# Values of four heads as one 512-column group, their gates as the next, with half of the values and results held in DRAM

## The chip, the core and the metric

The kernel runs on one core of a Trainium2 chip, in float32 data (matrix products in the chip's fp32r form, with operands split into a high and a low part). The metric is the device time in microseconds from launch to end. Before the change it is 775.31 us, the median of three runs (775.07 to 775.48).

## The reference

One layer of a mixer. `x` is 512 frames by 2048 channels.

```python
xn = rmsnorm(x, norm_gain)
q, k, v, g_sb, x_lru, g_lru = split(xn @ w_in, 6 parts of 1024 columns)
# 8 heads of 128: QK-norm, stick-breaking attention, strictly causal
w[t, s] = sigmoid(z[t, s]) * prod over s < j < t of (1 - sigmoid(z[t, j]))
y_sb  = (w @ v) * silu(g_sb)
# 8 groups of 128 channels: causal conv of width 4, two gate products, linear recurrence
y_lru = scan(conv(x_lru)) * silu(g_lru)
out = x + concat(y_sb, y_lru) @ w_out
```

## The kernel before, in words

**The loop.** The input projection is done in four rounds, p = 0 to 3, of two heads and two LRU channel groups each (line 528). A round has three groups of matmuls, each made by `in_group` (line 241) into four PSUM banks of the pool `ps_mm`, which has only those four: "qk" (queries and keys of two heads), "xg" (inputs and gates of two LRU groups) and "vg" (values and gates of two heads). A group runs over 8 chunks of the 2048 input channels; a chunk is one weight tile (`load_w`, line 223, two DMAs), split on ScalarE into a high part and on VectorE into a low part (`split_w`), and then three matmuls for each bank and each block of 128 channels: high by high, high by low, low by high.

**The vg group.** For queries, keys and gates the weights are stationary and 512 frames are streamed, so every matmul has 512 columns. Values are wanted with frames on the partitions, so there the frames are stationary and the weights are streamed; of the 512 weight columns of a vg group only 256 are values. So its first two banks are filled by matmuls of 256 columns, two halves to a bank (lines 278 to 289), and the other two banks, the gates, by matmuls of 512 (lines 292 to 294).

**After a vg group.** `finish_vg` (line 509) splits the values straight from PSUM into `vh`, `vl` and `v3` (lines 517 to 520), scales the two gate banks (`evac`, line 351), turns them into silu gates (`silu_gate`: three ScalarE steps, a VectorE step, a ScalarE step and a VectorE step, on one scratch tile `se` that all gates share with those of the LRU groups), makes the product of attention weights and values on TensorE (`attention_values`, lines 443 and 445) and multiplies it by the gate into `y_dram` (`gated`, line 364).

**The end of the loop and the output product.** `finish_vg(3)` and the scan of the last LRU group are put behind the first two weight splits of the output product (line 641). The products of heads 6, 7 and of LRU groups 6, 7 with their gates go straight into the tiles `yl` (line 648). The output product is done in the Strassen manner by seven products, in the order 1, 7, 5, 3, 6, 2, 4, each of 96 matmuls; each wants its weights split (line 619 on ScalarE, 620 on VectorE, 128x1024 at a time). The tiles `yl` go first into the sums for product 5 (lines 744 to 747).

**Order of the work.** Every engine works through its own list in order. The lists are laid out ahead by the framework's planner, which goes by its own estimate of durations and by the order of the program (`schedule_with_timeline_sim=True`); where an instruction waits, everything behind it on that engine waits too. Weight loads and results are issued on the queue of SyncE (SP); DMAs that add weights into DRAM run on the queue of GpSimd.

Of the kernel before, what the change touches and what calls it, by code (L numbers as in the profile page):

```python
# [9 lines left out]
F32 = mybir.dt.float32  # L10
# [12 lines left out]
def hybrid_block_kernel(ctx: ExitStack, tc: tile.TileContext, x, norm_gain, w_in, q_norm_gain,  # L23
# [7 lines left out]
    TT = S // P  # L31
    KC = 2
    WARM = 15
    FILL = 4
# [188 lines left out]
    def load_w(src, name):  # L223
        t = raw_pool.tile([P, KC, 512], F32, tag="raw", name=name)
        for s in range(2):
            last = nc.sync.dma_start(t[:, :, 256 * s:256 * s + 256], src[:, :, s, :])
        return t, last
# [12 lines left out]

    def in_group(a, p, vfirst, name, first=False):
        banks = [ps_mm.tile([P, 512], F32, tag="mm", name=f"{name}b{i}") for i in range(4)]
        NC = KT // KC

        def load(c):
            t, last = load_w(w_in_v[:, KC * c:KC * c + KC, a, :, 256 * p:256 * p + 256], f"{name}r{c}")
            if not first and c % 2 == 1 and sums:
                with tc.issue_after(last.ins):
                    sums.pop(0)()
            return t  # L250
# [8 lines left out]
        for c in range(NC):  # L259
# [13 lines left out]
            for b in range(4):  # L273
                for j in range(KC):
                    kt = KC * c + j
                    st, sp = kt == 0, kt == KT - 1
                    wh, wl = hl[j]
                    if vfirst and b < 2:
                        for u in range(2):
                            tt = 2 * b + u  # L280
                            o = banks[b][:, u * 256:(u + 1) * 256]
                            ts = slice(tt * P, (tt + 1) * P)
                            s0 = st and u == 0
                            nc.tensor.matmul(o, lhsT=xh[kt][:, ts], rhs=wh[:, 0:256], start=s0, stop=False,
                                             skip_group_check=True)
                            nc.tensor.matmul(o, lhsT=xh[kt][:, ts], rhs=wl[:, 0:256], start=False, stop=False,
                                             skip_group_check=True)
                            nc.tensor.matmul(o, lhsT=xl[kt][:, ts], rhs=wh[:, 0:256], start=False, stop=sp,
                                             skip_group_check=True)
                    else:  # L290
                        cs = slice(b * P, (b + 1) * P)
                        nc.tensor.matmul(banks[b], lhsT=wh[:, cs], rhs=xh[kt], start=st, stop=False)  # L292
                        nc.tensor.matmul(banks[b], lhsT=wh[:, cs], rhs=xl[kt], start=False, stop=False)  # L293
                        nc.tensor.matmul(banks[b], lhsT=wl[:, cs], rhs=xh[kt], start=False, stop=sp)  # L294
# [138 lines left out]

    def attention_values(h, wt, v, gate):
        hp = h % 2
# [9 lines left out]
        nc.tensor.matmul(o[:, 384:512], lhsT=v3[:, hs], rhs=w3, start=False, stop=True, skip_group_check=True)  # L445
        gated(h, o, gate)

# [60 lines left out]

    def finish_vg(p, banks, wts):
        vh = v_pool.tile([P, 3, 256], F32R, tag="vh", name=f"vh{p}")  # L510
        vl = v_pool.tile([P, 3, 256], F32R, tag="vl", name=f"vl{p}")
        v3 = v_pool.tile([P, 256], F32, tag="v3", name=f"v3{p}")
        for tt in range(TT):
            src = banks[tt // 2][:, (tt % 2) * 256:(tt % 2) * 256 + 256]
            r = rtok[:, tt:tt + 1]
            if tt == 3:
                nc.scalar.activation(v3, src, AF.Copy, scale=r)
                continue
            nc.scalar.activation(vh[:, tt, :], src, AF.Copy, scale=r)
            nc.vector.scalar_tensor_tensor(out=vl[:, tt, :], in0=src, scalar=r, in1=vh[:, tt, :].bitcast(F32),  # L520
                                           op0=ALU.mult, op1=ALU.subtract)
        v = (vh, vl, v3)
        gs = [evac(banks[2 + i], f"s{2 * p + i}") for i in range(2)]
        gates = [silu_gate(gs[i], f"s{2 * p + i}") for i in range(2)]
        for i in range(2):
            attention_values(2 * p + i, wts[i], v, gates[i])

    for p in range(4):
        banks = in_group(0, p, False, f"qk{p}", p == 0)
        banks = [evac(banks[i], f"qk{p}_{i}") for i in range(4)]  # L530
# [4 lines left out]
        wts = [attention_weights(2 * p + i) for i in range(2)]  # L535
        banks = in_group(2, p, False, f"xg{p}")
        xg = []
# [7 lines left out]
        for i in range(2):  # L545
            scans[i] = lru(2 * p + i, xg[i], xg[2 + i])
            if p < 3 or i == 0:
                scans[i]()
        banks = in_group(1, p, True, f"vg{p}")
        if p < 3:  # L550
            finish_vg(p, banks, wts)

# [88 lines left out]
    with tc.issue_after(last_hi[0].ins), tc.issue_after(last_lo[0].ins):  # L641
        scans[1]()
        finish_vg(3, banks, wts)
    for a in range(2):
        nc.sync.dma_start(yl[a], y_dram_a[1, :, a])
    for k in (14, 6, 15, 7):
        y, gate = late[k]
        nc.vector.tensor_tensor(out=yl[k % 4][:, k // 8], in0=y, in1=gate, op=ALU.mult)

    def product(i, banks, src, w):  # L650
# [171 lines left out]
```

## Time and profile before

| | |
|---|---|
| median of three runs | 775.31 us |
| the profiled execution | 775.84 us, of which the span of the instructions is 774.1 us |
| TensorE busy | 764.6 us |
| VectorE busy | 512.3 us |
| ScalarE busy | 440.5 us |
| DMA | 133.92 MB, mean 173 GB/s |

Times in the rows below count from the first instruction of the span. A duration of a matmul holds its way through the array, and the next one starts before it ends; what a matmul costs in a dense stretch is the distance from its start to the next start.

### The profile page before, as it was taken

The numbers are of one execution on the slowest core, as the hardware profiler recorded it, in microseconds if no ns is written. First come the engines' busy times: TensorE is split into PE (matmuls) and PEld (weight loads), VectorE is DVE, ScalarE is ACT, GpSimd is POOL, SyncE is SP. The second block draws the span as 40 slices with busy tenths as digits, with TensorE's granted clock in tenths as the row PEclk, the third lists the DMA queues.
The fourth block names the chain that finished last, engine by engine and source line by source line (L and its number), as shares of the span: only waits on it lengthen the run. The fifth ranks groups of instructions, "written<-read, shape, count | busy, mean of one in ns | idle before, by whom it ended". The sixth has DMA issues, their size and how long they took to land.

```text
span 774.1 us, 10702 instructions
## 1 busy us (share of the span) xinstructions
PE 764.6 (99%) x3853; PEld 647.5 (84%) x3853; DVE 512.3 (66%) x857; ACT 440.5 (57%) x828; POOL 37.4 (5%) x55
## 2 busy tenths in 40 slices
PE   8999999999999999999999999999999999999997
PEld 6888889988888899888889988888888878788886
DVE  4554587783445797725468976254787889976973
ACT  4934568582245777524469673245786766345541
POOL 0001101010101101001100000000000000000000
PEclk9999999999999999999999999999999999999999
DMA  9677876768987776788787523323145589898811
GB/s 287 208 167 141 198 165 163 172 148 215 185 203 144 197 154 177 148 227 193 164 200 145 149 90 123 108 85 106 55 133 168 151 340 315 227 290 200 262 63 55
DMA packets 92153, 133.92 MB, mean 173 GB/s; under 512 B 6258, under 2 KB 62148, under 8 KB 91844
## 3 DMA queue, kind: packets, MB, share of 16 engines
q1 hardware_dynamic: 83364, 116.45, 48.4%
q0 software_dynamic: 8704, 16.78, 18.1%
q8 instruction: 30, 0.49, 0.3%
q14 instruction: 23, 0.19, 0.1%
q10 hardware_dynamic: 32, 0.01, 0.0%
HBM read 125.87 MB, written 40.89 MB: 215 GB/s over the span
## 4 chain that ended last, share of the span: by engine, by line
PE 93%; DVE 5%; DMA 1%; issue 0%; SPq 0%; ACT 0%; DVEq 0%
PE p L679 5%; PE p L680 5%; PE p L678 5%; PE z L387 4%; PE qk0b L293 2%; PE qk0b L294 2%; PE xg0b L293 2%; PE xg3b L294 2%; PE xg1b L294 2%; PE xg2b L294 2%; PE xg0b L294 2%; PE xg3b L292 2%; PE xg2b L292 2%; PE xg1b L292 2%; PE xg0b L292 2%; PE xg1b L293 2%
## 5 line engine op out<-in xcount | busy, mean ns | idle before, releaser
L679 PE MATMUL p<-wo,os 128*128 128x512 f32 x192 | 74.9, 392 | 0.5 <-DVE wo L620 0.4
L680 PE MATMUL p<-wo,os 128*128 128x512 f32 x192 | 74.5, 390 | 0.0
L678 PE MATMUL p<-wo,os 128*128 128x512 f32 x192 | 69.5, 390 | 0.7 <-ACT wo L619 0.7
L619 ACT CAST wo<-c 128x1024 fp32r<-128x1024 f32 x44 | 46.2, 1051 | 35.6 <-PE p L680 33.9
L620 DVE TENSOR_TENSOR wo<-c,wo 128x1024 fp32r<-128x1024 f32 x44 | 53.4, 1222 | 13.4 <-ACT wo L619 13.4
L309 POOL DMA_DIRECT2D ws<-in_w_out_dram x32 | 33.8, 1055 | 371.4 <-DMA ws<-in_w_out_dram 185.0
L679 PEld LDWEIGHTS p<-wo,os 128*128 128x128 f32 x192 | 36.0, 188 | 9.6 <-DVE wo L620 2.3
L678 PEld LDWEIGHTS p<-wo,os 128*128 128x128 f32 x192 | 36.0, 188 | 8.6 <-ACT wo L619 1.1
L680 PEld LDWEIGHTS p<-wo,os 128*128 128x128 f32 x192 | 36.1, 188 | 7.4
L399 ACT ACTIVATE sp<-z 128x128 f32<-128x128 f32 (+3 forms) x32 | 13.9, 434 | 27.6 <-PE z L387 27.4
L293 PE MATMUL qk0b<-xl,hqk 128*128 128x512 f32 x64 | 26.4, 413 | 0.0
L294 PE MATMUL qk0b<-xh,lqk 128*128 128x512 f32 x64 | 25.2, 394 | 0.0
L293 PE MATMUL xg0b<-xl,hxg 128*128 128x512 f32 x64 | 25.2, 394 | 0.0
L292 PE MATMUL xg1b<-xh,hxg 128*128 128x512 f32 x64 | 25.2, 393 | 0.0
L292 PE MATMUL xg2b<-xh,hxg 128*128 128x512 f32 x64 | 25.2, 393 | 0.0
L292 PE MATMUL xg3b<-xh,hxg 128*128 128x512 f32 x64 | 25.1, 393 | 0.0
L292 PE MATMUL xg0b<-xh,hxg 128*128 128x512 f32 x64 | 25.1, 392 | 0.0
L293 PE MATMUL xg1b<-xl,hxg 128*128 128x512 f32 x64 | 25.1, 392 | 0.0
L293 PE MATMUL xg2b<-xl,hxg 128*128 128x512 f32 x64 | 25.1, 392 | 0.0
L293 PE MATMUL xg3b<-xl,hxg 128*128 128x512 f32 x64 | 25.1, 392 | 0.0
L294 PE MATMUL qk1b<-xh,lqk 128*128 128x512 f32 x64 | 25.0, 391 | 0.0
L292 PE MATMUL qk1b<-xh,hqk 128*128 128x512 f32 x64 | 24.9, 390 | 0.0
(542 smaller groups left out, 2377.4 us busy)
## 6 DMA issues: line engine op xcount, KB each, us to landing
ws<-in_w_out_dram POOLq DMA_DIRECT2D x32, 512.0 KB, 8.4
c<-ws SPq DMA_DIRECT2D x28, 512.0 KB, 5.2
ws<-in_w_out_dram SPq DMA_DIRECT2D x16, 512.0 KB, 6.8
ws<-ws SPq DMA_DIRECT2D x16, 512.0 KB, 6.4
c<-in_w_out_dram SPq DMA_DIRECT2D x16, 512.0 KB, 5.8
qk0r<-in_w_in_dram SPq DMA_DIRECT2D x16, 256.0 KB, 5.1
xg0r<-in_w_in_dram SPq DMA_DIRECT2D x16, 256.0 KB, 4.0
vg0r<-in_w_in_dram SPq DMA_DIRECT2D x16, 256.0 KB, 3.7
```

What stands on the lines that cost most here:

```text
L292: nc.tensor.matmul(banks[b], lhsT=wh[:, cs], rhs=xh[kt], start=st, stop=False)
L293: nc.tensor.matmul(banks[b], lhsT=wh[:, cs], rhs=xl[kt], start=False, stop=False)
L294: nc.tensor.matmul(banks[b], lhsT=wl[:, cs], rhs=xh[kt], start=False, stop=sp)
L309: nc.gpsimd.dma_start(wsum[i, m, a], block(*add, m, a), accum_op=ALU.add)
L387: nc.tensor.matmul(o, lhsT=lhsT, rhs=rhs, start=start, stop=stop, skip_group_check=True)
L399: nc.scalar.activation(e, z, AF.Abs)
L619: last_hi[0] = nc.scalar.copy(h, src)
L620: last_lo[0] = nc.vector.tensor_tensor(out=l, in0=src, in1=h.bitcast(F32), op=ALU.subtract)
L678: nc.tensor.matmul(bank, lhsT=sh[:, j, us], rhs=wh[:, j, :], start=st, stop=False)
L679: nc.tensor.matmul(bank, lhsT=sh[:, j, us], rhs=wl[:, j, :], start=False, stop=False)
L680: nc.tensor.matmul(bank, lhsT=sl[:, j, us], rhs=wh[:, j, :], start=False, stop=sp)
```

## The change

Values and gates of four heads, not two, are now gathered into groups. In round 0 (and 2) the third group is V: 512 columns of values of heads 0 to 3 (4 to 7), frames stationary, all matmuls of 512 columns, one bank to a block of 128 frames. In round 1 (and 3) it is G: the gates of the same four heads. In round 0 the values of heads 2 and 3 are scaled and written to DRAM (`v_dram`), and read back in round 1 before G is computed; the ungated results of heads 0 and 1 are written to DRAM (`o_dram`) and read back in round 1 to be multiplied by their gates. In round 2 the ungated results of heads 4 and 5 go to `y_dram` as they are, and are multiplied by their gates in the tiles `yl` at the end. A V or G weight tile comes by one DMA.

```diff
     def load_w(src, name):
         t = raw_pool.tile([P, KC, 512], F32, tag="raw", name=name)
+        if len(src.shape) == 3:
+            return t, nc.sync.dma_start(t, src)
...
-                    if vfirst and b < 2:
-                        for u in range(2):
-                            tt = 2 * b + u
-                            o = banks[b][:, u * 256:(u + 1) * 256]
-                            ts = slice(tt * P, (tt + 1) * P)
-                            s0 = st and u == 0
-                            nc.tensor.matmul(o, lhsT=xh[kt][:, ts], rhs=wh[:, 0:256], start=s0, stop=False,
-                                             skip_group_check=True)
...
+                    if a == V:
+                        ts = slice(b * P, (b + 1) * P)
+                        nc.tensor.matmul(banks[b], lhsT=xh[kt][:, ts], rhs=wh, start=st, stop=False)
+                        nc.tensor.matmul(banks[b], lhsT=xh[kt][:, ts], rhs=wl, start=False, stop=False)
+                        nc.tensor.matmul(banks[b], lhsT=xl[kt][:, ts], rhs=wh, start=False, stop=sp)
...
+    def finish_v(p, banks, wts):
+        scales = [rtok[:, tt:tt + 1] for tt in range(TT)]
+        v = split_v(p, [b[:, 0:256] for b in banks], scales)
+        for i in range(2):
+            t = wtile(f"vk{p}_{i}")[:, 0:512].rearrange("p (t c) -> p t c", t=2)
+            for u in range(2):
+                nc.scalar.activation(t[:, u, :], banks[2 * i + u][:, 256:512], AF.Copy, scale=scales[2 * i + u])
+            nc.sync.dma_start(v_dram[p // 2, i], t)
+        for i in range(2):
+            h = 2 * p + i
+            o = attention_values(h, wts[i], v)
+            t = y_pool.tile([P, S], F32, tag="y", name=f"o{h}")
+            nc.scalar.copy(t, o)
+            nc.sync.dma_start(o_dram[i] if h < 2 else y_dram[h], t)
+
+    def load_v(p):
+        srcs = []
+        for i in range(2):
+            t = wtile(f"vr{p}_{i}")[:, 0:512].rearrange("p (t c) -> p t c", t=2)
+            nc.sync.dma_start(t, v_dram[p // 2, i])
+            srcs += [t[:, 0, :], t[:, 1, :]]
+        return split_v(p, srcs, [1.0] * TT)
+
+    def finish_g(p, banks, wts, v):
+        gs = [evac(banks[i], f"s{2 * p - 2 + i}") for i in (2, 3, 0, 1)]
+        gates = [silu_gate(g, f"s{p}_{i}") for i, g in enumerate(gs)]
+        for i in range(2):
+            gated(2 * p + i, attention_values(2 * p + i, wts[i], v), gates[i])
+        for i in range(2):
+            h = 2 * p - 2 + i
+            if h > 1:
+                late[h] = gates[2 + i]
+                continue
+            t = y_pool.tile([P, S], F32, tag="y", name=f"or{h}")
+            nc.sync.dma_start(t, o_dram[i])
+            nc.vector.tensor_tensor(out=t, in0=t, in1=gates[2 + i], op=ALU.mult)
+            nc.sync.dma_start(y_dram[h], t)
...
-        banks = in_group(1, p, True, f"vg{p}")
-        if p < 3:
-            finish_vg(p, banks, wts)
+        if p % 2 == 0:
+            finish_v(p, in_group(V, p // 2, f"v{p}"), wts)
+        else:
+            v = load_v(p)
+            banks = in_group(G, p // 2, f"g{p}")
+            if p < 3:
+                finish_g(p, banks, wts, v)
...
         scans[1]()
-        finish_vg(3, banks, wts)
+        finish_g(3, banks, wts, v)
...
+    for k in (4, 5):
+        nc.vector.tensor_tensor(out=yl[k % 4][:, 0], in0=yl[k % 4][:, 0], in1=late[k], op=ALU.mult)
```

`split_v` is the splitting part of `finish_vg`, taken out as a function.

## Rows read from the trace of the kernel before

**Rows 1.** The page: busy time of each engine, and the chain of waits.
```profile
PE 764.6 (99%) x3853; PEld 647.5 (84%) x3853; DVE 512.3 (66%) x857; ACT 440.5 (57%) x828; POOL 37.4 (5%) x55
...
PE 93%; DVE 5%; DMA 1%; issue 0%; SPq 0%; ACT 0%; DVEq 0%
```

**Rows 2.** Waits of PE, whole span: us in total, times, longest us.
```profile
PE qk0b L292 <- DVE hqk L233: 1.8, 1, 1.8
...
PE p L678 <- ACT wo L619: 0.7, 1, 0.7
PE p L679 <- DVE wo L620: 0.4, 1, 0.4
```

**Rows 3.** Instruction groups by form, PE: busy us, mean ns; one value and one gate row.
```profile
L284 PE MATMUL vg0b<-hvg,xh 128*128 128x256 f32 x64 | 18.0, 283 | 0.0
...
L292 PE MATMUL vg0b<-xh,hvg 128*128 128x512 f32 x32 | 12.6, 393 | 0.0
```

**Rows 4.** Timeline of PE in the qk group of round 1: start us, us.
```profile
179.67 0.39 PE L294 MATMUL qk1b<-xh,lqk 128*128 128x512 f32 x1
...
185.79 0.39 PE L294 MATMUL qk1b<-xh,lqk 128*128 128x512 f32 x1
```

**Rows 5.** Timeline of PE, one chunk of the vg group of round 3.
```profile
599.22 0.28 PE L284 MATMUL vg3b<-hvg,xh 128*128 128x256 f32 x1
...
602.10 0.40 PE L292 MATMUL vg3b<-xh,hvg 128*128 128x512 f32 x1
...
604.84 0.28 PE L284 MATMUL vg3b<-hvg,xh 128*128 128x256 f32 x1
```

**Rows 6.** Busy time by stretch: length, PE, PEld, DVE, ACT, POOL, granted clock, DMA share.
```profile
166.00:315.00 149.00, 149.00 (x769) 127.38 (x769) 92.48 (x162) 85.54 (x164) 12.99 (x14) 1.00 0.79 179
...
611.00:637.00 26.00, 25.81 (x119) 21.05 (x117) 23.78 (x35) 17.24 (x27) 0.00 (x0) 1.00 0.93 321
...
637.00:659.00 22.00, 21.69 (x93) 17.42 (x94) 22.00 (x31) 13.91 (x18) 0.00 (x0) 1.00 0.88 299
```

**Rows 7.** Timeline of DVE around the boundary from round 1 to round 2.
```profile
321.43 0.69 DVE L238 TENSOR_TENSOR lqk<-qk2r,hqk 128x512 fp32r<-128x512 f32 x1
...
329.95 0.69 DVE L370 TENSOR_TENSOR y<-o,vs 128x512 f32<-128x512 f32 x1 [2.85 <-DMA y_dram<-y]
```

**Rows 8.** Timeline of DVE, end of round 3 and the first output products.
```profile
609.89 1.46 DVE L353 TENSOR_TENSOR vs<-vg3b,rbc 128x512 f32<-128x512 f32 x2
611.27 0.87 DVE L520 SCALAR_TENSOR_TENSOR vl<-vg3b,rtok,vh 128x256 fp32r<-128x256 f32 x2
...
622.03 1.23 DVE L620 TENSOR_TENSOR wo<-c__6127,wo 128x1024 fp32r<-128x1024 f32 x1 [1.41 <-ACT wo L619]
...
637.78 0.68 DVE L648 TENSOR_TENSOR yl__6116<-hl,vgl 128x512 f32<-128x512 f32 x1
638.38 0.68 DVE L358 TENSOR_TENSOR vs<-vs,es 128x512 f32<-128x512 f32 x1
...
645.93 0.69 DVE L710 TENSOR_TENSOR ye__6139<-yl__6118,ye__6139 128x512 f32<-128x512 f32 x1
...
650.07 0.69 DVE L710 TENSOR_TENSOR r<-r,e 128x512 f32<-128x512 f32 x1
...
661.30 0.68 DVE L620 TENSOR_TENSOR os<-ye__6139,os 128x512 fp32r<-128x512 f32 x1
```

**Rows 9.** Timeline of ACT in the same stretch.
```profile
605.72 0.62 ACT L344 ACTIVATE el<-vgl 128x512 f32<-128x512 f32 x1
...
615.22 0.47 ACT L517 ACTIVATE v<-vg3b,rtok 128x256 f32<-128x256 f32 x1
615.58 0.63 ACT L348 ACTIVATE el<-el 128x512 f32<-128x512 f32 x1
...
618.52 0.62 ACT L344 ACTIVATE es<-vs 128x512 f32<-128x512 f32 x1
...
629.96 0.62 ACT L344 ACTIVATE es<-vs 128x512 f32<-128x512 f32 x1
```

More of the change, by code (lines that the diff above doesn't have):

```diff
@@ L32, in hybrid_block_kernel @@
     KC = 2
+    V, G = (1, 0), (1, 1)
     WARM = 15
@@ L239, in split_w, with in_group @@
         return h, l
-    def in_group(a, p, vfirst, name, first=False):
+    def in_group(a, p, name, first=False):
         banks = [ps_mm.tile([P, 512], F32, tag="mm", name=f"{name}b{i}") for i in range(4)]
@@ L245, in load @@
         def load(c):
-            t, last = load_w(w_in_v[:, KC * c:KC * c + KC, a, :, 256 * p:256 * p + 256], f"{name}r{c}")
+            ks = slice(KC * c, KC * c + KC)
+            src = (w_in_v[:, ks, a[0], a[1], 512 * p:512 * p + 512] if isinstance(a, tuple) else
+                   w_in_v[:, ks, a, :, 256 * p:256 * p + 256])
+            t, last = load_w(src, f"{name}r{c}")
             if not first and c % 2 == 1 and sums:
@@ L277, in in_group @@
                     wh, wl = hl[j]
-                    if vfirst and b < 2:
-                        for u in range(2):
-                            tt = 2 * b + u
-                            o = banks[b][:, u * 256:(u + 1) * 256]
-                            ts = slice(tt * P, (tt + 1) * P)
-                            s0 = st and u == 0
-                            nc.tensor.matmul(o, lhsT=xh[kt][:, ts], rhs=wh[:, 0:256], start=s0, stop=False,
-                                             skip_group_check=True)
[L286 to L289, printed above, removed]
+                    if a == V:
[3 more added lines that the diff above has]
+                        nc.tensor.matmul(banks[b], lhsT=xl[kt][:, ts], rhs=wh, start=False, stop=sp)
                     else:
@@ L432, in attention_weights, with attention_values @@
         return wh, wl, w3
-    def attention_values(h, wt, v, gate):
+    def attention_values(h, wt, v):
         hp = h % 2
@@ L445, in attention_values @@
         nc.tensor.matmul(o[:, 384:512], lhsT=v3[:, hs], rhs=w3, start=False, stop=True, skip_group_check=True)
-        gated(h, o, gate)
+        return o
     def lru(g, xbank, gbank):
@@ L505, in lru_scan, with split_v @@
         gated(8 + g, y, silu_gate(gbank, n))
-    def finish_vg(p, banks, wts):
+    v_dram = dram.tile([2, 2, P, 2, 256], F32, name="v_dram")
+    o_dram = dram.tile([2, P, S], F32, name="o_dram")
+    def split_v(p, srcs, scales):
         vh = v_pool.tile([P, 3, 256], F32R, tag="vh", name=f"vh{p}")
@@ L512, in finish_vg @@
         v3 = v_pool.tile([P, 256], F32, tag="v3", name=f"v3{p}")
-        for tt in range(TT):
-            src = banks[tt // 2][:, (tt % 2) * 256:(tt % 2) * 256 + 256]
-            r = rtok[:, tt:tt + 1]
+        for tt, (src, r) in enumerate(zip(srcs, scales)):
             if tt == 3:
@@ L521, in finish_vg @@
                                            op0=ALU.mult, op1=ALU.subtract)
-        v = (vh, vl, v3)
-        gs = [evac(banks[2 + i], f"s{2 * p + i}") for i in range(2)]
-        gates = [silu_gate(gs[i], f"s{2 * p + i}") for i in range(2)]
+        return vh, vl, v3
+    def finish_v(p, banks, wts):
+        scales = [rtok[:, tt:tt + 1] for tt in range(TT)]
+        v = split_v(p, [b[:, 0:256] for b in banks], scales)
         for i in range(2):
-            attention_values(2 * p + i, wts[i], v, gates[i])
+            t = wtile(f"vk{p}_{i}")[:, 0:512].rearrange("p (t c) -> p t c", t=2)
[29 more added lines that the diff above has]
+            nc.sync.dma_start(y_dram[h], t)
     for p in range(4):
-        banks = in_group(0, p, False, f"qk{p}", p == 0)
+        banks = in_group(0, p, f"qk{p}", p == 0)
         banks = [evac(banks[i], f"qk{p}_{i}") for i in range(4)]
@@ L535, in hybrid_block_kernel @@
         wts = [attention_weights(2 * p + i) for i in range(2)]
-        banks = in_group(2, p, False, f"xg{p}")
+        banks = in_group(2, p, f"xg{p}")
         xg = []
```

## The prediction, made before the change was run

> **What bounds the kernel now.** I read four views in this order. First the page: TensorE is busy for 764.6 of 774.1 us and holds 93% of the chain that ended last [rows 1]. Second its waits: that view has only five lines, either at the start or in the output product, and the longest is 1.8 us [rows 2]. So a microsecond that TensorE does not need is a microsecond of the kernel, unless another engine is late just there. Third the timeline of TensorE, for what a matmul costs in a dense stretch. Fourth the busy time by stretch, for who could be late: in a round (149.00 us) VectorE works 92.48 us and ScalarE 85.54 us, so both have room; from 637 to 659 us, inside the output product, VectorE is busy for 22.00 of 22.00 us beside a TensorE busy for 21.69 [rows 6]. There both engines are at their end, and the change moves VectorE work towards that place.
>
> **The matmuls.** A group of rows stands for 64 matmuls; three such value groups in each of four rounds are 768 matmuls of 256 columns [rows 3]. They become 384 of 512 columns with the same product; the gates keep theirs. The means in those rows (283 and 393 ns) hold the way through the array and must not be subtracted. From start to start, 28 matmuls of 512 columns have 27 steps from 179.67 to 185.79: 0.2267 us each [rows 4]. In a chunk of a vg group 24 matmuls of 256 columns take 599.22 to 602.10, 0.1200 us each, and 12 of 512 take 602.10 to 604.84, 0.2283 us each [rows 5]. At the granted clock of 1.00 [rows 6], the 2.4 GHz level, 512 columns stream in 213.3 ns and 256 in 106.7: both kinds carry some 13.3 ns that do not depend on the columns, and 384 of these go. By rows: 24 x 0.1200 = 2.88 us a chunk becomes 12 x 0.2267 = 2.72, which saves 0.16; 8 chunks in 4 rounds are 32, so 5.1 us. With 0.2283 for the new ones it is 32 x 0.14 = 4.5; if the gate matmuls come down to 0.2267 as well, 5.62 less 24 x 0.2267 = 5.44 saves 0.18 a chunk, 5.8. I take 5.1, since a whole group of 512 columns is what rows 4 show.
>
> The Trainium skill puts this fixed part much lower: "TensorE: Matmul & The Clock Gate", in its section "Wait — 56ns, not 53.3ns?", gives about 2.5 ns a matmul at the warm clock. By it 384 fewer matmuls would save an estimated 1.0 us, not 5.1. The two rows of different width disagree with it for these operands.
>
> **Work moved in rounds 0 to 2.** Per pair of rounds the VectorE work is the same; it moves from the even round to the odd one. ScalarE gets four copies of 256 columns (0.47 us) and two of 512 (0.62) in an even round (such forms stand in rows 9), about 3.1 us, but loses two gates of four steps of 0.62 there, 5.0 us, to the odd one. After G in round 1 VectorE has two more scalings from PSUM (0.69 each: 609.89 to 611.27 for two [rows 8]), two more gates of two steps and two more products (0.60 each, the step from 637.78 to 638.38 [rows 8]), 5.0 us, less three value splits of 0.4 that now come before G: 3.8 us. Beside them stands the group qk2, 43 us of TensorE (192 x 0.2267) in which VectorE owes only its 16 weight splits of 0.6; a split every few microseconds is what it must not miss [rows 7]. That cover is worth up to 3.8 us if it were gone. I take 0.3 us, and keep 0 to 2.
>
> Each bank of V waits for two ScalarE copies and a VectorE split before the next group can use it. Bank 0 is done 18 matmuls (4.1 us) before the group ends and is wanted again only after the next group's start, so two copies of 0.47 and a split of 0.4 fit. In G the banks are listed as 2, 3, 0, 1. If VectorE kept that order, bank 0 would come free two scalings after the end, 1.4 us; the products of weights and values for two heads, which TensorE can then do at once, cover it.
>
> **New waits.** The result copies on ScalarE wait for one of two `y` tiles. Before, VectorE stood 2.85 us for such a tile [rows 7]; behind ScalarE's copy would stand the casts of the next group's weights, and behind them TensorE, for which four split tiles (line 52), two chunks of 5.4 us, are in hand. So nothing is charged; without that cover the 2.85 us would be paid once or twice. On SP the store of `v_dram` waits for copies, with the next group's weight loads queued behind it, four of which are already in; V and G loads are one DMA in place of two, so SP has less to issue. `load_v` is ready a whole round ahead.
>
> **The end of round 3.** This is the term that decides. The same 3.8 us of VectorE work, two late products of 0.60 for heads 4 and 5 counted in it, comes after the last input group; ScalarE gets eight gate steps less four value copies, 8 x 0.62 - 4 x 0.47, 3.1 us, in a stretch where it is busy for 17.24 of 26.00 [rows 6]. From 611 to 637 us VectorE has 26.00 - 23.78 = 2.2 us free, from 637 none [rows 6]. If 2.2 is filled, 1.6 us is left over. Against that, TensorE starts the two heads' products at once, about 3.5 us in which no output weight need be split, and VectorE may put off work that nobody wants yet: eight `r` operations of 0.6 such as the one at 650.07, whose results are wanted only when product 5 is done [rows 8].
>
> Then there is the chain of the gates, since all pass one scratch tile in turn. The LRU gate starts at 605.72, head 6 at 618.52, head 7 at 629.96 and ends at 638.38 + 0.68 = 639.06 [rows 8, 9]: 12.8, 11.4 and 9.1 us each. Heads 4 and 5 now follow. At 9.1 to 11.4 each they end at 657.3 to 661.9. The late product and the first sum (0.69 each) make 658.7 to 663.3, and the split that feeds product 5 with head 5's tile stands at 661.30 now, after a sum at 645.93 [rows 8]. So the 15 us of cover are used up: 0 to 2.0 us late. The price of this stage is thus between -1.1 (the waits of 0.7 and 0.4 in rows 2 gone, as splits leave the stretch) and 9.8 (below). I take 1.6, the overflow of VectorE, with the chain just in time.
>
> **Sum.** -5.1 + 0.3 + 1.6 = -3.2 us against the profiled execution, 775.84, so 772.6; that execution lies 0.5 above the median of 775.31, where I expect 772.1.
>
> **Rivals.** (a) All of the gain stays: the planner fills VectorE's free 2.2 us, `r` operations give way, the gates come in time. For it: TensorE's waits are short and the added work is small. Against it: 22.00 of 22.00. Time: 775.31 - 5.1 = 770.2, down to 769 with the -1.1.
>
> (b) The gain is nearly given back: VectorE pays its whole 3.8 us in the full stretch, and 0.8 elsewhere: -0.5, 774.8, no change that can be measured. For it: lists are in fixed order, and after 637 there is no free time.
>
> (c) Slower, by the gate chain. If all four gates take the LRU gate's 12.8 us, head 5's ends at 618.52 + 51.2 = 669.7, its sum at 671.1, 9.8 us after 661.30; TensorE waits at product 5. The net is +4.7, 780.0. It decides from 12.0 us a gate on (6.65 us late, 5.1 of gain plus 1.55). For it: more VectorE and ScalarE work between the steps makes each gate longer, and ScalarE's order mixes them with weight casts that wait for TensorE. Against: the last two gates took 11.4 and 9.1, and no output weight tile comes free during the first 3.5 us.
>
> (d) The change doesn't do what it says: a V matmul of 512 columns, with split weights streaming, costs as much as two of 256, 0.240 us. Then nothing is saved and 1.9 is paid: 777.2. For it: no row shows 512 columns of split weights against stationary frames in the groups. Against it: 27 equal steps of 0.2267 with the operands the other way round [rows 4], and equal fixed parts at both widths. With the figure of the Trainium skill's page named above ("TensorE: Matmul & The Clock Gate", same section) the estimate would be 776.2.
>
> **Chances.** Forecast (770.8 to 773.7) 0.46, (a) 0.16, (b) 0.21, (c) 0.14, (d) 0.03. A change under 0.2%, 1.55 us, can't be told from none. Faster: 0.46 + 0.16 = 0.62; the same: (b), 0.21; slower: 0.14 + 0.03 = 0.17. The range, 769.4 to 776.9, holds the forecast, (a) but for its lowest end, and (b); it leaves out (c), (d) and a few hundredths below.
>
> **What would show it.** In the profile after, steps of 0.227 us through V, and 4.5 to 5.8 us less from the start of round 0's V to the end of G in round 3; no wait of TensorE at the boundaries of the rounds; in the output product, the waits of lines 678 and 679 grown to about 2.5 us, VectorE full until some 4 us later, and head 5's late product ahead of the split for product 5. The prediction is wrong if V's steps are longer, if TensorE waits at a boundary for banks or splits, or if the `yl` products of heads 4 and 5 end a chain of waits of several microseconds.

## The result, and the profile after

The changed kernel takes 783.80 us (median of 4 runs, 783.08 to 785.20) against 775.25 (775.07 to 775.48): 1.011 times, 95% interval 1.0098 to 1.0122. It is 8.5 us slower; forecast were 772.1 us and a range that ends at 776.9. The profiled execution took 783.73 us, its span 782.0.

The page after has 384 matmuls fewer than [rows 1], and the chain that ended last has less of TensorE in it and more of DMA and of SP's queue:

```profile
PE 762.5 (98%) x3469; PEld 628.5 (80%) x3469; DVE 514.6 (66%) x857; ACT 444.8 (57%) x840; POOL 37.1 (5%) x55
...
PE 89%; DVE 5%; DMA 3%; SPq 1%; issue 1%; ACT 0%; DVEq 0%
```

TensorE's timeline shows that the saving is there. In V of round 0 there are 24 equal steps from the first to the second row below, 0.2267 us each as in [rows 4], and in round 3 the last matmul of G starts at 605.92, where the last of before's value group started at 610.24:

```profile
155.86 0.39 PE L290 MATMUL v0b<-hv,xl 128*128 128x512 f32 x1
...
161.30 0.40 PE L290 MATMUL v0b<-hv,xl 128*128 128x512 f32 x1
...
605.92 0.40 PE L295 MATMUL g3b<-xh,lg 128*128 128x512 f32 x1
```

So 4.3 us are won by there. From that matmul to the last of the output product (777.42) it is 171.50 us; before it was 159.05 (610.24 to 769.29). These 12.45 us are the loss, and they lie behind the last input group; 12.45 - 4.32 = 8.1 is the difference of the spans (782.0 and 774.1) to 0.2. I call this stretch the tail; every run below is read by it.

TensorE's waits, us in total, times, longest. The last two lines answer to lines 678 and 679 in [rows 2]; the first is new, and so are two of the three behind the second line:

```profile
PE p L722 <- ACT e L775: 8.2, 1, 8.2
PE p L723 <- DVE wo L662: 2.9, 3, 1.6
...
PE p L722 <- ACT wo L661: 0.7, 1, 0.7
```

These add up to the loss: 8.2 + 2.9 + 0.7, and 1.6 for matmuls at the lower clock behind the long stand (last section), less the 1.1 that [rows 2] have for these two lines, are 12.3 of the 12.45 us.

Where the long one stands, on TensorE's timeline, and what follows it:

```profile
645.80 0.39 PE L724 MATMUL p<-wo,os 128*128 128x512 f32 x1
654.44 0.80 PE L722 MATMUL p<-wo,os 128*128 128x512 f32 x1 [8.25 <-ACT e L775]
655.03 0.63 PE L723 MATMUL p<-wo,os 128*128 128x512 f32 x1
655.46 0.63 PE L724 MATMUL p<-wo,os 128*128 128x512 f32 x1
```

This is product 7. Its second half goes into the banks of product 1, and these are free when ScalarE has copied product 1's results out (`e1`, line 775). ScalarE's timeline after, from the first gate step of each gate on the scratch tile to those copies:

```profile
612.69 1.05 ACT L661 CAST wo<-c__5746 128x1024 fp32r<-128x1024 f32 x1 [7.62 <-PE p L724]
620.49 0.63 ACT L345 ACTIVATE es<-vs 128x512 f32<-128x512 f32 x1
627.20 0.62 ACT L345 ACTIVATE es<-vs 128x512 f32<-128x512 f32 x1
638.53 0.63 ACT L345 ACTIVATE es<-vs 128x512 f32<-128x512 f32 x1
648.64 0.63 ACT L345 ACTIVATE es<-vs 128x512 f32<-128x512 f32 x1 [1.37 <-DVE vs L359]
652.31 0.63 ACT L349 ACTIVATE es<-es 128x512 f32<-128x512 f32 x1 [1.72 <-DVE es L348]
652.85 2.03 ACT L775 COPY e<-p 128x512 f32<-128x512 f32 x4
```

And before, where they follow on the last of two gates, with the last product that VectorE writes into a tile `yl` (a late product) beside them:

```profile
640.72 0.68 DVE L648 TENSOR_TENSOR yl__6116<-o,vs 128x512 f32<-128x512 f32 x1
...
641.35 2.03 ACT L731 COPY e<-p 128x512 f32<-128x512 f32 x4
```

In both kernels the four copies stand behind the last gate's last step on ScalarE, and within 0.9 us of VectorE's last late product (640.72 before, 653.70 after, below), though they read nothing of either. The gates of heads 6, 7, 4 and 5 start at 620.49, 627.20, 638.53 and 648.64, one after another, and the copies move from 641.35 to 652.85 with them. TensorE wanted them at 646.

The windows that answer to [rows 6] show the stall, and the granted clock (0.84 in the second, the number behind GpSimd's):

```profile
611.00:637.00 26.00, 23.95 (x102) 18.33 (x101) 22.93 (x33) 18.94 (x28) 0.00 (x0) 1.00 0.84 302
637.00:659.00 22.00, 13.75 (x53) 10.67 (x52) 21.80 (x30) 12.29 (x18) 0.00 (x0) 0.84 0.81 244
```

VectorE's end of the chain, and what is late behind it: head 5's gate and late product, then the `r` operations, which stand for the loads of x, in front of the splits for product 5. Head 4's is at 667.30 (657.75 before), head 5's at 669.03, where [rows 8] have it at 661.30; the weight split between them ends the wait of 1.6 us:

```profile
652.97 0.69 DVE L359 TENSOR_TENSOR vs<-vs,es 128x512 f32<-128x512 f32 x1
653.70 0.69 DVE L692 TENSOR_TENSOR yl__5728<-yl__5728,vs 128x512 f32<-128x512 f32 x1
...
664.71 1.41 DVE L754 TENSOR_TENSOR r<-r,e 128x512 f32<-128x512 f32 x2 [1.90 <-DMA r<-in_x_dram]
667.30 0.69 DVE L662 TENSOR_TENSOR os<-ye__5751,os 128x512 fp32r<-128x512 f32 x1
...
669.03 0.68 DVE L662 TENSOR_TENSOR os<-ye__5749,os 128x512 fp32r<-128x512 f32 x1
```

### The profile page after: what moved, and what is told of

It reads as the page before. It is cut to its first block, busy times and chain, and to the rows that moved or that the text cites. A ratio compares the mean times of both kernels' runs of the same rounds, so it can differ in the third digit from the quotient of the medians.

```text
span 782.0 us, 9877 instructions
## 1 busy us (share of the span) xinstructions
PE 762.5 (98%) x3469; PEld 628.5 (80%) x3469; DVE 514.6 (66%) x857; ACT 444.8 (57%) x840; POOL 37.1 (5%) x55
## 4 chain that ended last, share of the span: by engine, by line
PE 89%; DVE 5%; DMA 3%; SPq 1%; issue 1%; ACT 0%; DVEq 0%
PE p L723 5%; PE p L724 5%; PE p L722 5%; PE z L388 4%; PE qk0b L294 2%; PE v2b L290 2%; PE g1b L295 2%; PE v0b L290 2%; PE xg0b L294 2%; PE qk0b L295 2%; PE xg2b L295 2%; PE xg3b L295 2%; PE g1b L293 2%; PE xg1b L295 2%; PE v0b L289 2%; PE v2b L288 2%
## 5 line engine op out<-in xcount | busy, mean ns | idle before, releaser
L722 PE MATMUL p<-wo,os 128*128 128x512 f32 x192 | 72.3, 394 | 8.9 <-ACT e L775 8.2
L723 PE MATMUL p<-wo,os 128*128 128x512 f32 x192 | 75.3, 394 | 1.7 <-DVE wo L662 1.7
L724 PE MATMUL p<-wo,os 128*128 128x512 f32 x192 | 74.9, 392 | 0.0
L403 DVE SCALAR_TENSOR_TENSOR sp<-z,sp 128x128 f32<-128x128 f32 (+3 forms) x32 | 15.5, 485 | 15.4 <-ACT sp L402 15.3
L290 PE MATMUL v2b<-hv,xl 128*128 128x512 f32 x64 | 25.4, 397 | 0.0
L293 PE MATMUL g3b<-xh,hg 128*128 128x512 f32 x64 | 25.2, 394 | 0.0
L290 PE MATMUL v0b<-hv,xl 128*128 128x512 f32 x64 | 25.2, 394 | 0.0
L295 PE MATMUL g3b<-xh,lg 128*128 128x512 f32 x64 | 25.1, 395 | 0.0
L289 PE MATMUL v0b<-lv,xh 128*128 128x512 f32 x64 | 25.1, 392 | 0.0
```

The costliest lines, as they stand in the source:

```text
L289: nc.tensor.matmul(banks[b], lhsT=xh[kt][:, ts], rhs=wl, start=False, stop=False)
L290: nc.tensor.matmul(banks[b], lhsT=xl[kt][:, ts], rhs=wh, start=False, stop=sp)
L722: nc.tensor.matmul(bank, lhsT=sh[:, j, us], rhs=wh[:, j, :], start=st, stop=False)
L723: nc.tensor.matmul(bank, lhsT=sh[:, j, us], rhs=wl[:, j, :], start=False, stop=False)
L724: nc.tensor.matmul(bank, lhsT=sl[:, j, us], rhs=wh[:, j, :], start=False, stop=sp)
```

## The experiments

Three theories stood against each other. *Place*: the copies could go earlier, but the planner lists them behind the gates, since their pool (`res`) takes over space of the gates' pool (`wk`). *Room*: VectorE is full in the tail, and 3.8 us more of work make its splits late wherever the copies stand. *Chain*: four gates in a row end too late for product 5, which reads what they gate (rival (c)). The expectations use letters, and not always the same letter for the same theory, so go by what a text says behind the letter. All medians of before, taken anew beside these runs, lie between 775.29 and 775.62. Times in brackets behind a median are lowest and highest; ratios are to before, with 95% intervals.

### The copies' place, in the whole change

`e1_own_pool`: the four copies get a space of their own.

```diff
+    e_pool = ctx.enter_context(tc.tile_pool(name="e1p", bufs=4, reuse_waits="tile"))
...
-        return r_pool.tile([P, 512], F32, tag=tag, name=name)
+        return (e_pool if tag == "e1" else r_pool).tile([P, 512], F32, tag=tag, name=name)
```

> The changed kernel, with the four tiles e1 (results of product 1, copied out of PSUM) in a pool of their own that shares no space with the pool of the gates. Theory A (order and space): the planner lists the e1 copies behind the last gate only because their pool shares space with the gates' pool; freed of that, they come after product 1 and TensorE's wait of 8.2 us goes, with some 1.4 us of half clock behind it: 783.8 - 9.6 = 774.2. Theory B (the gate chain feeds product 5, as rival (c) had it): the wait only moves to product 5, where head 5's tile is wanted: about 781 to 783. Theory C (VectorE is overfull by 3.8 us): the wait moves to weight splits, 778 to 782.

Measured: 778.38 us (778.17 to 779.95), ratio 1.0044 [1.0029, 1.0059]; tail 166.3. The copies moved to 620.6 to 634, their wait is gone, and 5.4 us came back. TensorE's waits now:

```profile
PE p L723 <- DVE wo L662: 3.9, 3, 2.3
...
PE p L722 <- ACT wo L661: 1.1, 1, 1.1
PE p L724 <- DVE os L662: 0.8, 1, 0.8
```

Place is thus one cause, shown, and not the only one. What the run shows is that a pool of their own moves the copies. That the shared space is why the planner had listed them late is a reading of the program and not shown; at run time they waited for nothing, since in the changed kernel the first starts at 652.85, before VectorE has made its last late product (653.70).

`e2_scratch`: four scratch tiles, so that the gates need not pass one in turn. `e3_both`: both edits.

```diff
+        tags = ("se", "qn", "we", "ae") if p == 3 else ("se",) * 4
-        gates = [silu_gate(g, f"s{p}_{i}") for i, g in enumerate(gs)]
+        gates = [silu_gate(g, f"s{p}_{i}", tags[i]) for i, g in enumerate(gs)]
```

> The changed kernel, with each of the four gates of round 3 on a scratch tile of its own (tiles that attention no longer uses), so the gates need not go one after the other; VectorE and ScalarE have the same work. Theory A: the last gate is done some 10 us earlier, the e1 copies are listed earlier and the loads of x for the sums come in time: 783.8 - 8.2 - 1.4 - 1.7 = 772.5. Theory B: the same, about 772 to 773. Theory C: the work is the same, so 779 to 783.

> Both edits: own pool for e1 and four scratch tiles. Theory A: as with the scratch tiles alone, or a little less, since the copies no longer depend on the gates at all: 771 to 772.5. Theory B: 772 to 773. Theory C: 778 to 782.

Measured: 780.44 (780.06 to 780.91), 1.0067 [1.0052, 1.0082], and 778.64 (778.43 to 779.62), 1.0046 [1.0031, 1.0061]. In `e2_scratch` the wait for the copies is gone as well (they start at 642.70). With free scratch the gates run early, and TensorE waits for weight splits instead, which I read as the gates having taken their places on VectorE and ScalarE; of `e2_scratch`:

```profile
PE p L724 <- DVE wo L663: 6.6, 7, 1.4
PE p L723 <- ACT wo L662: 2.0, 2, 1.3
```

So the shared scratch tile is not what costs, as the prediction's chain had it: unchaining the gates only changes which wait is paid.

### Half of the change, and the two gates left out

`e4_half`: V and G in rounds 0 and 1 only; rounds 2 and 3 keep their value and gate group as before.

```diff
-        if p % 2 == 0:
+        if p > 1:
+            banks = in_group(1, p, f"vg{p}", vfirst=True)
+            if p < 3:
+                finish_vg(p, banks, wts)
+        elif p % 2 == 0:
             finish_v(p, in_group(V, p // 2, f"v{p}"), wts)
```

> The change in rounds 0 and 1 only; rounds 2 and 3 have the value and gate groups of before, and so the end of round 3 is that of before. If all of the loss lies at the end of round 3 (theories A, B and C alike), half of the saving is left: 192 fewer matmuls, in the traces 2 x 1.1 us, so 775.25 - 2.2 = 773.0. If the stores to and loads from DRAM or the boundaries of rounds cost something, 775 or more.

`e5_no_gates45`: the whole change without gates and late products of heads 4 and 5; the output takes these two heads ungated.

```diff
-        gs = [evac(banks[i], f"s{2 * p - 2 + i}") for i in (2, 3, 0, 1)]
+        gs = [evac(banks[i], f"s{2 * p - 2 + i}") for i in ((2, 3) if p == 3 else (2, 3, 0, 1))]
...
-    for k in (4, 5):
-        nc.vector.tensor_tensor(out=yl[k % 4][:, 0], in0=yl[k % 4][:, 0], in1=late[k], op=ALU.mult)
```

> The changed kernel without the gates of heads 4 and 5 (their two scalings, two silu gates and two late products are left out; the output of these heads is not gated). All that the end of round 3 has more than before is gone, the matmuls are all there. If the loss is these gates (their place in the lists, theory A, and their work on VectorE, theory C): 775.25 - 4.4 = 770.9. If something else at the end of the loop costs (the products of heads 6 and 7 in one block ahead of product 1, or the reads from DRAM): 774 or more.

Measured: half 773.56 (772.57 to 774.29, 9 runs), 0.9975 [0.9965, 0.9985]; its last input group ends 2.3 us earlier than before's, its tail is 159.06 to before's 159.05, and its waits are those of [rows 2]:

```profile
PE p L744 <- ACT wo L685: 0.7, 1, 0.7
PE p L745 <- DVE wo L686: 0.4, 1, 0.4
```

Without the two gates 772.91 (772.42 to 776.58, 9 runs), 0.9976 [0.9964, 0.9989], tail 160.9: 10.6 of the 12.45 us are the two gates'. The rest is one wait of 2.3 us for a weight split, which `e16_no45_own` (below) explains.

### Orders that did not help

`e6_order`: `e3_both`, and the cast of product 1's third weight tile, for which ScalarE stood 7.62 us at 612.69 with gate steps queued behind it, is put behind the last gate's logarithm.

```diff
+                with tc.issue_after(last_ln[0].ins) if (i, m, a) == (1, 0, 2) else nullcontext():
+                    wh, wl = ready.pop(("w", m, a)) if ("w", m, a) in ready else split_w_out(i, m, a, w[m, a])
```

> The kernel with own pool and four scratch tiles (778.64), with ScalarE's cast for the third weight tile of product 1 put behind the last gate's third step. In the trace of the changed kernel ScalarE stands 7.6 us before that cast, with the gate steps behind it, and VectorE is idle for 4.3 us. Theory D (that standing is what VectorE lacks later): 778.64 - 4 = 774.5. Theory C alone (VectorE has too much to do): 778 to 779.

Measured 782.34 (781.73 to 783.15), 1.0087 [1.0072, 1.0102]: TensorE then waits 5.7 us, until 621.07, for that very weight. `e7_swap`: in round 3 heads 4 and 5 are gated out of the group before, and the gates of the two LRU tiles come out of the last. `e8_swap_free`: the same with own space and four scratch tiles.

```diff
+            if a == XS:
+                src = w_in_v[:, ks, 2, 0, 768:1024], w_in_v[:, ks, 1, 1, 512:768]
+            if a == GS:
+                src = w_in_v[:, ks, 1, 1, 768:1024], w_in_v[:, ks, 2, 1, 768:1024]
```

> The changed kernel with gates exchanged between the last two groups of round 3: heads 4 and 5 are gated from the third-last, LRU groups 6 and 7 from the last. After the last group VectorE has two scalings and one gate more than before, less three value splits: 1.4 us more, not 3.8; four gates, not five, pass the scratch tile after it. Theory A: the last gate is done some 10 us earlier than in the changed kernel, so most of the 9.6 us goes: 774 to 776. Theory C: 2.4 of the 3.8 us of VectorE work go: 781.

> The exchange of gates together with the own pool for e1 and a scratch tile for each gate. Theories A and C together: the gain of 4.4 less about 1.4 us of VectorE work: 772.3. If theory D holds, that ScalarE's cast stands in front of the gates here too, 775 to 777.

Measured 780.62 (779.68 to 780.77), 1.0062 [1.0047, 1.0077], and 778.21 (777.93 to 778.59), 1.0034 [1.0020, 1.0047]: `e8_swap_free` takes what `e3_both` takes to 0.4 us, and `e7_swap` 3.2 us less than the changed kernel, with waits for weight splits of up to 2.5 us and none for the copies. Other gates behind the last group do not bring the gain back either. `e9_gpsimd`: `e3_both` with four products of the gates of heads 4 and 5 on GpSimd.

```diff
-        nc.vector.tensor_tensor(out=g, in0=g, in1=e, op=ALU.mult)
+        (nc.gpsimd if pool else nc.vector).tensor_tensor(out=g, in0=g, in1=e, op=ALU.mult)
```

> The kernel with own pool and four scratch tiles (778.64), with the four products for the gates of heads 4 and 5 (gate by value, and the late product) on GpSimd, which does nothing in this stretch. Theory C (after the copies and the chain are out of the way, what is left is VectorE work): 2.4 us less on VectorE, 776 to 776.5. If VectorE's load is not what is left, or GpSimd slows VectorE by as much as it takes over: 778.5 or more.

Measured 779.81 (778.51 to 780.44), 1.0055 [1.0041, 1.0069], no gain over `e3_both`. The window from 611 us has GpSimd at 10.21 us for four products:

```profile
611.00:637.00 26.00, 20.71 (x79) 15.18 (x77) 22.73 (x28) 21.66 (x35) 10.21 (x4) 0.93 0.72 267
```

That is 2.55 us each in the mean, where VectorE takes 0.6.

### The suspected cost alone, without the rest of the change

`e10_half_dve`: the half version with six products of 0.6 us on VectorE behind the last group, which nobody reads. `e11_half_gates`: the half version that makes two gates a second time there, their results unused. `e12_half_own`: the half version with the copies' own space.

```diff
+            t = wtile("extra")[:, 0:512]
+            for _ in range(6):
+                nc.vector.tensor_tensor(out=t, in0=gs[0], in1=gs[1], op=ALU.mult)
```

```diff
+            extra = [evac(banks[2 + i], f"x{i}") for i in range(2)]
+            late[4], late[5] = [silu_gate(g, f"x{i}") for i, g in enumerate(extra)]
...
+    for k in (4, 5):
+        nc.vector.tensor_tensor(out=late[k], in0=yl[k % 4][:, 0], in1=late[k], op=ALU.mult)
```

> The half change (773.56) with six VectorE products of 0.6 us, whose result nobody reads, after the scalings of the last gates: the cost of 3.6 us of VectorE work at that place by itself, with no chain, no ScalarE work and no late release of space. Theory C: 773.56 + 2 to 3.6 = 775.6 to 777.2. If the planner can give way (work that is not urgent is put off): 773.6 to 774.5.

> The half change with the gates of heads 6 and 7 made a second time at the end of round 3, each multiplied by a column block of yl and not used further: the suspected cost alone (two scalings, two gates on the one scratch tile, two late products, their tiles held as long), with the matmuls and the rest of round 3 as before. Theory A with C: the copies of e1 are listed behind these gates, as in the changed kernel: 773.56 + 10 to 12 = 784 to 786. If the loss needs the G group itself: 774 to 777.

> The half change with the own pool for e1, looked at as a version to keep. In its trace the e1 copies come in time, so theory A expects the same as the half change, 773.56 within 0.5; lower only if the waits of 0.6 and 0.85 us in the output product go too (772.1).

Measured: 784.86 (782.90 to 784.96), 1.0116 [1.0102, 1.0130]; 788.85 (788.15 to 789.31), 1.0171 [1.0155, 1.0186]; 773.57 (772.97 to 775.50, 11 runs), 0.9977 [0.9969, 0.9986]. So 3.6 us of VectorE work cost 11.3 us, and two unused gates 15.3, more than the whole change loses. Of the first, the copies on ScalarE, the waits, and a stand of VectorE for a load of x:

```profile
647.59 2.04 ACT L801 COPY e<-p 128x512 f32<-128x512 f32 x4
```

```profile
PE p L749 <- DVE wo L690: 4.5, 2, 4.0
PE p L748 <- ACT e L801: 2.6, 1, 2.6
```

```profile
663.93 0.69 DVE L780 TENSOR_TENSOR r<-r,e 128x512 f32<-128x512 f32 x1 [3.45 <-DMA r<-in_x_dram]
```

And of the second:

```profile
657.56 2.03 ACT L803 COPY e<-p 128x512 f32<-128x512 f32 x4
```

```profile
PE p L750 <- DVE f L782: 13.2, 1, 13.2
```

In `e10` the last gate's last step on ScalarE is at 638.74, long before the copies. In all eight kernels in which the copies have no pool of their own, they start within 1.6 us of VectorE's last late product, whichever that is (in `e11` an unused one):

| kernel | last late product, us | copies, us |
|---|---|---|
| before | 640.72 | 641.35 |
| `e4_half` | 638.39 | 638.67 |
| `e5_no_gates45` | 641.48 | 639.95 |
| `e2_scratch` | 641.87 | 642.70 |
| `e10_half_dve` | 648.42 | 647.59 |
| `e7_swap` | 652.05 | 652.78 |
| after | 653.70 | 652.85 |
| `e11_half_gates` | 658.41 | 657.56 |

So it is the last late product, more than the last gate, that the copies go with. The late products are the last to read tiles of the pools that the program closes just ahead of `res`, which fits Place without proving the reason. Whether such a price is Room or Place, two more runs tell: `e13_dve_own` and `e14_gates_own` are these two kernels with the own space, the diff of `e1_own_pool`.

> The kernel e10_half_dve (half of the change, and six VectorE products of 0.6 us behind the last input group, 784.86 us, 11.3 over e4_half's 773.56) with a space of its own for the four copies of product 1. Theory A (most of the 11.3 us is the place of these copies, and what it does to the work listed behind them): the wait of 2.6 us for the copies goes, and the time falls to at most 773.6 + 3.6 + 1 = 778. Theory B (VectorE has no slack in this stretch, and an extra microsecond there makes splits late wherever the copies stand): 780 to 784, with the waits on VectorE's splits of lines 690 and 691 at 4 us or more. In both TensorE ends no sooner than in e4_half.

> The kernel e11_half_gates (half of the change, and two gates made a second time behind the last input group, 788.85 us, 15.3 over e4_half) with the same own space for the copies of product 1. Theory A: the wait of 13.2 us on the additions f, which stand behind the copies, goes; what is left is the work of two gates, 4 VectorE steps of 0.6 us and two scalings of 0.69, 3.8 us, and the 3.1 of ScalarE beside it: 775 to 779. Theory B: 781 to 786, the wait on f replaced by waits on splits. e1_own_pool, the same cure in the whole change, left 3 us over before and 7.5 over what it should have come to without any loss (770.9), so A by itself is not expected to bring e14 to e4_half's time.

Measured: 772.52 (772.17 to 772.99), 0.9961 [0.9946, 0.9976], and 772.96 (772.27 to 775.48, 10 runs), 0.9970 [0.9960, 0.9979]. Both prices, 11.3 and 15.3 us, are gone to nothing, though the work is still done; I had expected some 3 us to stay. The copies of `e13` stand where the data allow, and its waits in the output product are 0.7 and 0.2:

```profile
622.06 0.59 ACT L802 COPY e<-p 128x512 f32<-128x512 f32 x1 [0.68 <-PE p L750]
...
635.09 0.59 ACT L802 COPY e<-p 128x512 f32<-128x512 f32 x1
```

```profile
PE p L748 <- ACT wo L689: 0.7, 1, 0.7
...
PE p L749 <- DVE wo L690: 0.2, 1, 0.2
```

Room has fallen: a VectorE busy for 22.00 of 22.00 us has room for 3.6 more, if others may give way; `e13` and `e14` have 22.00 of 22.00 in that stretch too. What was left of `e1_own_pool` had to be something that may not give way.

### The chain

`e15_unread`: `e1_own_pool`, with the late products of heads 4 and 5 written where nobody reads them, so that the output takes the two heads ungated. `e16_no45_own`: `e5_no_gates45` with the own space.

```diff
-        nc.vector.tensor_tensor(out=yl[k % 4][:, 0], in0=yl[k % 4][:, 0], in1=late[k], op=ALU.mult)
+        nc.vector.tensor_tensor(out=late[k], in0=yl[k % 4][:, 0], in1=late[k], op=ALU.mult)
```

> The kernel e1_own_pool (778.38 us), with the products of heads 4 and 5 and their gates made as they are, but written to the gate's tile and not to the tile that the output product reads, so that nothing waits for them: the output takes the two heads ungated. The work is the same, to the instruction. Theory C (what is left of the loss is the chain of four gates, of which product 5 needs the last, head 5's at 659.98): 771 to 773.5, TensorE's tail 158 to 161 us. Theory B (it is the work itself, 3.8 us of VectorE in a stretch without slack): 776 to 779.

> The kernel e5_no_gates45 (772.91; the gates of heads 4 and 5 are left out, and the output takes the two heads ungated) with the own space for the copies of product 1. It is what the whole change would take if the two gates cost nothing. By the matmuls saved, 4.3 us in the group ends, 775.6 - 4.3 = 771.3 at a tail of 159; if the tail shortens as it did in the two half kernels with an own space (158.0, against 159.1): 770.2. If the wait of 2.43 us for a weight split at 639 in e5_no_gates45 is not a matter of the copies' place: 772.9 as before.

Measured: 771.61 (770.93 to 772.66), 0.9954 [0.9937, 0.9971], tail 159.6; 771.01 (770.73 to 771.45), 0.9942 [0.9928, 0.9957], tail 158.9; the wait of 2.3 us that `e5_no_gates45` has is gone in `e16`. With the same instructions and only the need taken away, and a list that the planner makes for that, `e15` is 6.8 us faster than `e1_own_pool`. Its last late product stands 7.75 us behind the last split for product 5, and may:

```profile
659.38 0.68 DVE L662 TENSOR_TENSOR os<-ye__5745,os 128x512 fp32r<-128x512 f32 x1
...
667.13 0.69 DVE L692 TENSOR_TENSOR vs<-yl__5728,vs 128x512 f32<-128x512 f32 x1
```

In `e1_own_pool` the same product is at 659.98; two sums, four `f`, a weight split and three more sums follow before head 5's split at 667.24. TensorE's longest wait ends not with that split but with the weight split ahead of it, which stands behind the four `f`:

```profile
659.98 0.68 DVE L692 TENSOR_TENSOR yl__5728<-yl__5728,vs 128x512 f32<-128x512 f32 x1
...
661.91 2.47 DVE L754 TENSOR_TENSOR f<-p,e 128x512 f32<-128x512 f32 x4
664.30 1.21 DVE L662 TENSOR_TENSOR wo<-c,wo 128x1024 fp32r<-128x1024 f32 x1
...
667.24 0.68 DVE L662 TENSOR_TENSOR os<-ye__5749,os 128x512 fp32r<-128x512 f32 x1
```

```profile
665.57 0.50 PE L723 MATMUL p<-wo,os 128*128 128x512 f32 x1 [2.28 <-DVE wo L662]
```

Before it, from 657 on, TensorE waits 0.80 for head 4's split, 1.14 for a weight cast and 0.33 for the cast of head 5's tile. The four waits are 4.55 us, and the nine steps from 666.60 to 670.25, at the 1.2 GHz level, take 1.6 more than 9 x 0.2267: 6.2 of the 6.8 us.

Two runs then tried to give the chain time in the whole change. `e17_45_first`: the gates in the order 4, 5, 6, 7, since product 5 takes the tiles so. `e18_p5_order`: the gates as they were, and product 5 taking the tiles in the order 6, 7, 4, 5.

```diff
+        order_g = (2, 3, 0, 1) if p == 1 else (0, 1, 2, 3)
+        gs = {i: evac(banks[i], f"s{2 * p - 2 + i}") for i in order_g}
+        gates = {i: silu_gate(gs[i], f"s{p}_{i}") for i in order_g}
+        gates = [gates[i] for i in (2, 3, 0, 1)]
```

```diff
+        seq = (2, 3, 0, 1) if i == 5 else range(NA)
-            for a in range(NA):
+            for a in seq:
...
-    c5 = load_sum(5)
+    c5 = load_sum(5, [(m, a) for m in range(2) for a in (2, 3, 0, 1)])
```

> The kernel e1_own_pool with the four gates in another order: heads 4 and 5, then 6 and 7, since product 5 takes the tiles in the order 4, 5, 6, 7 (the split of head 4's tile feeds its first matmuls). Theory C: head 7's tile is then the last, and the matmuls of three tiles (12 of 0.227 us each for one half, 8.2 us together) stand ahead of it in product 5: the waits of 656 to 663 go, 772 to 775. Theory B: no gain, 777.5 to 779.

> The kernel e1_own_pool (gates in the order 6, 7, 4, 5), with product 5 taking the tiles in the order 6, 7, 4, 5 too, and its weights loaded in that order, so that head 5's tile, whose late product stood at 659.98 and whose split at 667.24, comes last in product 5 and heads 6 and 7 leave their banks early. Theory C (the chain of the gates ends late for what product 5 wants first): the waits of 656 to 663 shrink from 5.2 us by the three tiles of 2.7 us that now stand ahead, to 2 at most: 773 to 775.5. If what is listed ahead of head 5's split on VectorE (four f, four sums) makes the wait, whatever the order of the tiles: 776 to 778.5.

Measured: 777.54 (777.14 to 778.71, 9 runs), 1.0028 [1.0018, 1.0038], and 779.59 (778.72 to 779.76), 1.0056 [1.0039, 1.0072]; neither as hoped. In `e17` the wait went from the tile to a bank: head 7's attention result stays in PSUM until its gate, now the last, has multiplied it, and product 5 begins in that bank.

```profile
PE p L724 <- DVE yl__5726 L694: 4.0, 1, 4.0
```

In `e18` head 5's split is no earlier (668.17), but TensorE wants it later, and in the stretch that `e1_own_pool` stumbled in TensorE is busy for 13.00 of 13.00 us from 659 (9.25 there):

```profile
659.00:672.00 13.00, 13.00 (x59) 10.78 (x58) 13.00 (x19) 6.43 (x8) 0.00 (x0) 1.00 0.93 254
```

but then a weight split of product 5 stands behind `r` operations, at 680.59, and TensorE waits for it:

```profile
PE p L724 <- DVE wo L662: 6.6, 3, 4.9
```

So the order of the tiles does take the chain off the path, and the list that the planner makes for it puts another wait there. No order was found in which the whole change keeps its gain; among the kernels with the whole output and no added work, the half version (with or without the own space) is the one that beats both before and after.

## Why the prediction was wrong

**The matmuls: right.** Steps of 0.2267 us were forecast and found. Forecast with the boundaries were -5.1 + 0.3 = -4.8 by the end of round 3; measured -4.3 here, and the ends of G in ten other kernels with V and G in all rounds (605.00 to 606.62) give -5.2 to -3.6. Rival (d) is out. So is the estimate of 1.0 us from the Trainium skill's "TensorE: Matmul & The Clock Gate", section "Wait — 56ns, not 53.3ns?": the trace does not agree with it for these operands.

**Boundaries and new waits: right.** TensorE's list of waits has nothing between the first group of round 0 and the output product.

**The end of round 3: the step that failed.** The term was +1.6, its upper bound 9.8; it measured +12.45. Of the signs that I had named, the waits of lines 678 and 679 came (2.9 and 0.7, 3.6 us, where 2.5 was expected); the stand of 8.2 us on the copies was not among them, nor among the signs of being wrong. Taken apart by runs that each differ in one edit, with the planner's lists made anew for each: after to `e1_own_pool`, 5.4 us, the place of the copies; `e1_own_pool` to `e15`, 6.8, the need of product 5 for the two late products, with the chain of gates ahead of them; `e15` to `e16`, 0.6, the work of two gates itself (no more than the spread of either). The sum is 12.8, from medians; the tail of `e16` is 158.9 to 159.05 before.

The term was sized by the wrong thing. "If 2.2 is filled, 1.6 us is left over" counts VectorE's work against its idle time; that work was worth 0.6, although 22.00 of 22.00 is what the window says, since `r` operations gave way, as rival (a) said: in `e15` the first stands at 672.13, before at 650.07. A wait for the copies of product 1 was not in the sum at all. Rival (b), Room, is out by `e13` and `e14`.

Rival (c), which I gave 0.14, came nearest: it has the kernel slower, by the gates. But its mechanism, gates that each take 12.8 us, did not occur; that its 780.0 lies on the right side of before is in part luck. Gates on one scratch tile took 6.7, 11.3 and 10.1 us from start to start (620.49, 627.20, 638.53, 648.64), one below the 9.1 to 11.4 of my forecast and two within it; head 5's ended at 653.7, earlier than the 657.3 to 661.9 that I thought just in time. Its place was wrong too: not the split for product 5, but first the copies of product 1, which go with the last late product. [Rows 9] could not show it, since I had cut them at the gates; the row at 641.35, with copies that wait for no gate and stand behind one and beside a late product, was in the trace of before and asked for a reason. With the copies out of the way the chain was late for product 5 after all: in `e1_own_pool` head 5's late product and first sum end at 661.4, within the 658.7 to 663.3 of my forecast, but I had put its split right behind them, and nine more operations stand between, with a weight split that TensorE waits for among them. So the chain as such came when I said; what it cost came from the list behind it and from product 5 taking heads 4 and 5 first.

What stays open: why the planner lists the copies with the last late product, which of its costs put the weight split of `e18` so late, and whether the whole change can be listed to take 771; it was not reached.

## What to carry to other kernels

An operation that waits for no data can still be late, because it is listed behind something late; here a space of its own freed it. Before work is added at the end of a chain, look at what is listed behind its last step, and ask whether data or space put it there. Work on a full engine is cheap where other work may give way and dear where it feeds the next product: to tell one from the other, keep the instructions and take away the reader. A loss can be two waits one behind the other, of which the profile shows the first; the second comes out when the first is cured.

## What the hardware showed beside that

After the 8.25 us stand the granted clock falls: the matmuls from 655.03 on start 0.43 us apart, the 1.2 GHz level, before steps of 0.23 come back, and the window has 0.84. The eight steps from 654.44 to 657.89 take 3.45 us where 8 x 0.2267 = 1.81 were due, so 1.6 us come on top of the stand. The same follows the waits of 4.0 us in `e17` and 4.9 in `e18`: counted in the same way, 12 steps from 661.10 to 666.34 cost 2.5 us, and 11 from 681.86 to 686.69 cost 2.3.
